# One core, one decoder layer: operand tiles at multiples of 512 bytes, output pieces crosswise in PSUM, x loaded another way

## The chip, the core and the metric

The kernel runs on one core of a Trainium2 chip. A core has TensorE (PE in the rows, with its weight loads as PEld), VectorE (DVE), ScalarE (ACT), GpSimd (POOL) and SyncE (SP); here SyncE only issues DMA transfers, and ScalarE has a DMA queue of its own. The metric is the device time of one execution in microseconds, as the median of several runs.

## What is computed

One layer of a hybrid decoder on 256 tokens of 1024 features. All inputs of the five mixer branches come from one product `h = x @ w_in + b_in`; the branches' gated outputs are merged, projected and normalized.

```python
h = x @ w_in + b_in                       # (256, 12690), split into a, b, c, d, e, z, merge
o_a = moba_attention(aq, ak, av)          # 6 heads of 64, causal at this length
o_b = dilated_mixture(bqk, bv)            # three dilations, one softmax
o_c = forgetting_attention(cq, ck, cv, log_sigmoid(c_f))
o_d = rms(gated_delta_rule(conv(d_qkv), beta, g)) * gdn_norm_w
o_e = memory_cross_attention(e_q, layer_norm(mem), w_mem_kv)
o = stack([o_a, o_b, o_c, o_d, o_e]) * silu(z)
y = sum(sigmoid(merge_logits) * einsum('bsnc,ncd->bsnd', o, w_branch), axis=2)
out = layer_norm(2 ** 0.25 * x + y @ w_out, ln_g, ln_b)
```

## The kernel before

Every large product is made of three matmuls in the type float32r: each operand is split into a part `hi` (rounded by ScalarE, L123) and a rest `lo` (a subtraction on VectorE, L124), and the products hi x hi, hi x lo and lo x hi are summed in PSUM (`mm3`, L126; every such matmul carries line L128). The tokens are kept split for the whole program in `xhi` and `xlo` (128 partitions, 8 chunks of features, 256 tokens, L140).

Weights come in units of up to 1024 columns of 4 bytes per partition (`Unit`, L163): a DMA into one of five `raw` buffers, a split into one of four `hi` and four `lo` buffers, then the matmuls. The loop at L1120 walks the units in the order of `ORDER` and keeps some loads and splits ahead. In a feature-major unit (`fm_unit`) the weights are the stationary operand and 256 tokens of xhi or xlo stream past (rows `mm<-xhi,hi`). In a token-major unit (`tm_block`) the weights stream, 384 or 402 columns, past stationary tokens (rows `mm<-hi,xhi`). The merge units stream a branch's gated output, an `f` tile of pool `f3`; the unit `mk` streams the normalized memory, in a `big` tile. Attention, convolution and the delta rule run as side streams that are stepped between the units.

The program's first block is the token-major product with `wcs` (value of branch c and its scalars). It loads and splits x piece by piece beside its own weights (`load_x` L278, `split_x` L286); x goes through two of the five `raw` buffers, all on SyncE's queue. The constants that its evacuation needs (`vcb`, `bcol` and others, `consts` at L303) are issued as a side stream among them. Matmul results of this kind lie in three `mm` buffers in PSUM.

The last product, with `w_out`, has five pieces: for token half t = 0 two of 512 columns, for t = 1 one of 512 and two of 256 (`PC`, L1021). Two `lg` tiles of two banks each take the first four (L1036: tile t holds both pieces of t), an `mm` buffer the fifth. `finish` (L1050) ends each piece with its last 15 matmuls, adds the residual on VectorE (L1071) and takes statistics (L1072); `norm` (L1054) then normalizes and stores a token half.

What stands where in memory follows from the order in which the pools are made: `cpool` with xhi, xlo and all constants first, then `wpool` (raw, hi, lo), `f3`, `big` and `sp`. In the program as built xhi and xlo start 128 bytes past a multiple of 512, and raw, hi, lo, f3 and big tiles 192 past. The order of instructions on an engine is made by a scheduler from dependencies and program order; `keep` pins an instruction to its place in program order.

Of the kernel before, what the change touches and what calls it, by code (L numbers as in the profile page):

```python
# [15 lines left out]
P = 128  # L16
S = 256
# [58 lines left out]
@with_exitstack  # L76
def kernel(ctx: ExitStack, tc: tile.TileContext, T: dict, out: bass.AP):
    nc = tc.nc
    cpool = ctx.enter_context(tc.tile_pool(name="cpool", bufs=1))
    wpool = ctx.enter_context(tc.tile_pool(name="wpool", bufs=3))  # L80
    f3 = ctx.enter_context(tc.tile_pool(name="f3", bufs=16))
    big = ctx.enter_context(tc.tile_pool(name="big", bufs=2))
    sp = ctx.enter_context(tc.tile_pool(name="sp", bufs=4))
    ps = ctx.enter_context(tc.tile_pool(name="ps", bufs=2, space=bass.MemoryType.PSUM))
    dr = ctx.enter_context(tc.tile_pool(name="dr", bufs=1, space=bass.MemoryType.DRAM))
# [6 lines left out]
    def nm(s):  # L92
        uid[0] += 1
        return f"{s}_{uid[0]}"

    def bigt(shape, dt=F32):
        return big.tile(shape, dt, tag="big", name=nm("big"))
# [7 lines left out]
    def ct(name, shape, dt=F32):  # L105
        return cpool.tile(list(shape), dt, name=name)
# [7 lines left out]
    def lgps():  # L114

        return pst("lg", (P, 2, 512), 2)
# [2 lines left out]
        return pst("av", shape, 1)  # L119


    def split(hi, lo, src):
        A_.activation(hi, src, AF.Copy)  # L123
        V_.tensor_tensor(lo, src, hi.bitcast(F32), op=ALU.subtract)  # L124

    def mm3(pt, lh, ll, rh, rl, first, last, pin=False):  # L126
# [10 lines left out]
    HR = (slice(0, 64), slice(64, 128))  # L137


    xhi, xlo = ct("xhi", (P, KD, S), F32R), ct("xlo", (P, KD, S), F32R)  # L140
    cst = ct("cst", (P, C_N))
    vb, vcb = ct("vb", (P, 2, BW)), ct("vcb", (P, BW + 18))
    bcol = ct("bcol", (P, T["bcol"].shape[1]))
# [19 lines left out]
    class Unit:  # L163
# [7 lines left out]
        def load(self):  # L171
            self.r = wpool.tile([P, 1024], F32, tag="raw", name=nm("raw"), bufs=NRAW)
            for i, p in enumerate(self.parts):
                if self.before is not None:
                    self.before[0](i, len(self.parts))
                nc.sync.dma_start(self.r[:, p], self.src[:, p])

        def split(self):
            self.h = wpool.tile([P, 1024], F32R, tag="hi", name=nm("hi"), bufs=NHI)
            self.l = wpool.tile([P, 1024], F32R, tag="lo", name=nm("lo"), bufs=NHI)  # L180
            for i, p in enumerate(self.parts):
                if self.before is not None:
                    self.before[1](i, len(self.parts))
                split(self.h[:, p], self.l[:, p], self.r[:, p])

    def need(name):
        while name is not None and name not in done:
# [88 lines left out]
    xraw = {}  # L276

    def load_x(i, j, n):  # L278
        if i % 2 == 0 and j == 0:
            xraw["t"] = wpool.tile([P, 4, S], F32, tag="raw", name=nm("raw"), bufs=NRAW)  # L280
        w = 2 // n
        o = 2 * i + w * j
        xraw[i, j] = xraw["t"][:, o % 4:o % 4 + w]
        nc.sync.dma_start(xraw[i, j], T["xT"][:, o:o + w])

    def split_x(i, j, n):  # L286
        w = 2 // n
        o = 2 * i + w * j
        split(xhi[:, o:o + w], xlo[:, o:o + w], xraw[i, j])

    def evac_c(p, t):
        if t == 0:
# [10 lines left out]
    def consts():  # L303
        for _ in range(CW):
            yield 1
        nc.sync.dma_start(vcb, T["vcb"].to_broadcast([P, BW + 18]))
        nc.sync.dma_start(bcol, T["bcol"])
        nc.sync.dma_start(cw, T["convw"])
        nc.sync.dma_start(adt, T["adt"].to_broadcast([P, 12]))
        nc.sync.dma_start(cst[:, :C_MA], T["cst"][:, :C_MA])  # L310
        flag("consts")


# [6 lines left out]
    def scalars():  # L320

        yield from wait("sc")
        nc.sync.dma_start(cst[:, C_MA:], T["cst"][:, C_MA:])
        nc.sync.dma_start(gnw, T["gnw"])
        nc.sync.dma_start(mgb, T["mgb"])
        nc.sync.dma_start(vb, T["vb"].to_broadcast([P, 2, BW]))

        V_.tensor_scalar(cwh, cw, 0.5, None, op0=ALU.mult)
        hb = bcol[:, 3 * len(FM):]
        V_.tensor_scalar(hb, hb, 0.5, None, op0=ALU.mult)  # L330
        for n, f in [("z" + i, 0.5) for i in BR] + list(QSCALE.items()):
            i = FM.index(n) * 3
            V_.tensor_scalar(bcol[:, i:i + 3], bcol[:, i:i + 3], f, None, op0=ALU.mult)
        flag("bias")
        yield
        a, lp = ct("a", (P, 2, 12)), ct("lp", (P, 2, 12))
        e, s1, s2, ea = ct("e", (P, 24)), ct("s1", (P, 24)), ct("s2", (P, 24)), ct("ea", (P, 6))
        for t in range(2):
            V_.tensor_scalar(a[:, t, 0:6], sc[:, t, 0:6], -1.0, None, op0=ALU.mult)
            V_.tensor_tensor(a[:, t, 6:12], sc[:, t, 6:12], adt[:, 6:12], op=ALU.add)  # L340
        af, lpf = a.rearrange("p t c -> p (t c)"), lp.rearrange("p t c -> p (t c)")
        V_.scalar_tensor_tensor(e, af, -1.0, af, op0=ALU.mult, op1=ALU.max)
        A_.activation(beta, sc[:, :, 12:18], AF.Exp, scale=-1.0)
        A_.activation(ea, adt[:, 0:6], AF.Exp)
        yield
        A_.activation(e, e, AF.Exp, scale=-1.0)
        V_.tensor_scalar(beta, beta, 1.0, None, op0=ALU.add)
        V_.reciprocal(beta, beta)
        V_.tensor_scalar(ea, ea, -1.0, None, op0=ALU.mult)
        yield  # L350
        V_.tensor_scalar(s1, e, 2.0, None, op0=ALU.add)
        V_.reciprocal(s1, s1)
        V_.tensor_tensor(s1, s1, e, op=ALU.mult)
        V_.tensor_tensor(s2, s1, s1, op=ALU.mult)
        V_.tensor_scalar(lpf, s2, 2.0 / 17, None, op0=ALU.mult)
        for n in (15, 13, 11, 9, 7, 5, 3):
            V_.scalar_tensor_tensor(lpf, lpf, 2.0 / n, s2, op0=ALU.add, op1=ALU.mult)
        V_.scalar_tensor_tensor(lpf, lpf, 2.0, s1, op0=ALU.add, op1=ALU.mult)
        V_.scalar_tensor_tensor(lpf, af, 0.0, lpf, op0=ALU.max, op1=ALU.add)
        yield  # L360

        for t in range(2):
            V_.tensor_scalar(fg[:, t, 0:6], lp[:, t, 0:6], -1.0, None, op0=ALU.mult)
            V_.tensor_tensor(lp[:, t, 6:12], lp[:, t, 6:12], ea, op=ALU.mult)
            V_.tensor_scalar(fg[:, t, 6:12], lp[:, t, 6:12], MAGIC, -MAGIC, op0=ALU.add, op1=ALU.add)
            V_.tensor_tensor(fg[:, t, 12:18], lp[:, t, 6:12], fg[:, t, 6:12], op=ALU.subtract)
        yield BURST

        lg = lgps()
        pt, p2 = lg[:, 0, :36].rearrange("p (t c) -> p t c", t=2), lg[0:18, 1, :S]  # L370
        keep(PE.matmul(pt[:, 0], K(C_TRI), fg[:, 0], start=True, stop=True))
        keep(PE.matmul(pt[:, 1], K(C_ONE), fg[:, 0], start=True, stop=False))
        keep(PE.matmul(pt[:, 1], K(C_TRI), fg[:, 1], start=False, stop=True))
        keep(PE.matmul(p2, fg[:, 0], K(C_TRI, 256), start=True, stop=False))
        keep(PE.matmul(p2[:, P:], fg[:, 1], K(C_TRI), start=False, stop=True))
        yield
        V_.tensor_scalar(ngt, pt, -1.0, None, op0=ALU.mult)
        grow = ct("grow", (18, S))
        V_.tensor_copy(grow, p2)
        R["gscr"] = dr.tile([18, S], F32, name="gscr")  # L380
        yield
        nc.sync.dma_start(R["gscr"], grow)
        flag("scalars")
# [635 lines left out]
    def out_units():  # L1019
# [12 lines left out]

        def chunk(u, k, t):
            if k == 0 and t == 0:
                lgs = [lgps() for _ in range(2)]
                fin["p"] = [[lg[:, i] for i in range(2)] for lg in lgs]  # L1036
                fin["p"][1].append(mmps((P, 512)))
                warm = spt("warm", (P, 1), bufs=1)
                A_.activation(warm, yhl[2][0][:, 1, 0:1].bitcast(F32), AF.Sqrt, scale=0.0, bias=0.0)
            if k < 3:  # L1040
                for i in range(len(PC[t])):
                    out_mm(u, k, t, i, k == 0, False)
            elif t == 0:
                late.append((u, k))
# [5 lines left out]
        def finish():  # L1050
# [3 lines left out]
            def norm(t):  # L1054
                V_.bn_aggr(mv[:, t], st2[t].rearrange("p c s -> p (c s)"))
                rs = rstd[:, t:t + 1]
                V_.tensor_scalar(rs, mv[:, t, 1:2], LN_EPS, None, op0=ALU.add)
                A_.activation(rs, rs, AF.Sqrt)
                V_.reciprocal(rs, rs)
                for c, cs in enumerate((slice(0, 512), slice(512, 1024))):  # L1060
                    o = xres[:, t, cs]
                    V_.scalar_tensor_tensor(o, o, mv[:, t, 0:1], lngb[:, 0, cs], op0=ALU.subtract, op1=ALU.mult)  # L1062
                    V_.scalar_tensor_tensor(o, o, rs, lngb[:, 1, cs], op0=ALU.mult, op1=ALU.add)  # L1063
                    (nc.sync, nc.scalar)[c].dma_start(out[t * P:(t + 1) * P, cs], o)
# [148 lines left out]
```

## Time and profile before

| | us |
|---|---|
| median of 3 runs (468.28 to 470.16) | 469.86 |
| the profiled execution | 469.32 |
| its span, first to last instruction | 467.2 |
| TensorE busy | 449.9 |
| VectorE busy | 328.1 |
| ScalarE busy | 265.5 |

A row of the profile names line, engine, operation and tiles as out<-in. Matmuls overlap in their pipeline, so the duration of one (some 280 ns) says little; what counts is the step from one start to the next. The granted clock is 0.994 of full speed over the whole span.

### The profile page before, as it was taken

The numbers are of one execution on the slowest core, as the hardware profiler recorded it, in microseconds if no ns is written. First come the engines' busy times: TensorE is split into PE (matmuls) and PEld (weight loads), VectorE is DVE, ScalarE is ACT, GpSimd is POOL, SyncE is SP. The second block draws the span as 40 slices with busy tenths as digits, with TensorE's granted clock in tenths as the row PEclk, the third lists the DMA queues.
The fourth block names the chain that finished last, engine by engine and source line by source line (L and its number), as shares of the span: only waits on it lengthen the run. The fifth ranks groups of instructions, "written<-read, shape, count | busy, mean of one in ns | idle before, by whom it ended". The sixth has DMA issues, their size and how long they took to land. (4 is left out here: it accounts for less than half of the span.)

```text
span 467.2 us, 10262 instructions
## 1 busy us (share of the span) xinstructions
PE 449.9 (96%) x4039; PEld 425.0 (91%) x4039; DVE 328.1 (70%) x757; ACT 265.5 (57%) x520; POOL 30.6 (7%) x36
## 2 busy tenths in 40 slices
PE   6999999999999999999999989999989999999993
PEld 3999999999998999999999989988989999999963
DVE  4799998877797535564655689895676565587746
ACT  5466685765666644444434976694684654475600
POOL 0000020010000000000000112100022112200000
PEclk9899999999999999999999999999999999999999
DMA  7978577555445545566434165564765445678202
GB/s 253 380 246 255 164 225 252 159 178 173 125 130 160 152 125 172 176 202 183 125 109 126 60 176 182 173 193 152 250 201 184 145 150 148 190 234 278 91 0 90
DMA packets 35051, 81.38 MB, mean 174 GB/s; under 512 B 8970, under 2 KB 17468, under 8 KB 34876
## 3 DMA queue, kind: packets, MB, share of 16 engines
q1 hardware_dynamic: 34715, 80.22, 55.8%
q8 instruction: 31, 0.51, 0.4%
q10 hardware_dynamic: 288, 0.52, 0.3%
q14 instruction: 17, 0.13, 0.1%
HBM read 79.37 MB, written 1.36 MB: 173 GB/s over the span
## 5 line engine op out<-in xcount | busy, mean ns | idle before, releaser
L124 DVE TENSOR_TENSOR lo<-raw,hi 128x1024 fp32r<-128x1024 f32 (+4 forms) x163 | 169.3, 1040 | 83.4 <-ACT hi L123 80.8
L128 PE MATMUL mm<-xhi,hi 128*128 128x256 f32 x776 | 219.5, 283 | 1.2 <-DVE yt L993 1.2
L128 PE MATMUL mm<-xhi,lo 128*128 128x256 f32 x776 | 216.1, 279 | 1.3 <-DVE lo L124 1.3
L128 PE MATMUL mm<-xlo,hi 128*128 128x256 f32 x776 | 216.5, 279 | 0.0
L123 ACT ACTIVATE hi<-raw 128x1024 fp32r<-128x1024 f32 (+4 forms) x163 | 146.0, 899 | 111.9 <-PE mm L128 83.5
L128 PEld LDWEIGHTS mm<-xhi,hi 128*128 128x128 f32 x776 | 146.3, 189 | 5.8 <-issue 2.7
L128 PEld LDWEIGHTS mm<-xhi,lo 128*128 128x128 f32 x776 | 145.8, 188 | 1.8 <-DVE lo L124 1.7
L128 PEld LDWEIGHTS mm<-xlo,hi 128*128 128x128 f32 x776 | 146.0, 188 | 0.8 <-issue 0.8
L128 PE MATMUL mm<-f,hi 128*128 128x256 f32 x240 | 44.7, 282 | 0.7 <-ACT th L976 0.7
L994 POOL TENSOR_TENSOR yacc<-yacc,yt 128x256 f32<-128x256 f32 x24 | 24.4, 1018 | 280.0 <-DVE yt L993 275.2
L128 PEld LDWEIGHTS mm<-f,hi 128*128 128x128 f32 x240 | 36.6, 188 | 1.6 <-ACT th L976 1.3
L128 PE MATMUL mm<-f,lo 128*128 128x256 f32 x120 | 33.7, 281 | 0.0
L128 PEld LDWEIGHTS mm<-f,lo 128*128 128x128 f32 x120 | 22.6, 188 | 0.0
L128 PE MATMUL mm<-hi,xhi 128*128 128x384 f32 (+1 forms) x48 | 16.6, 363 | 2.1 <-ACT hi L123 2.1
L135 PE MATMUL lg<-f,f 64*128 64x256 f32 (+2 forms) x192 | 18.5, 354 | 0.0
L976 ACT ACTIVATE th<-mm,bcol 128x256 f32<-128x256 f32 x40 | 18.5, 462 | 0.0
L768 ACT ACTIVATE pr<-pr,mm 128x128 f32<-128x128 f32 (+1 forms) x36 | 15.9, 443 | 4.5 <-DVE mm L759 4.5
L128 PE MATMUL mm<-lo,xhi 128*128 128x384 f32 (+1 forms) x48 | 17.3, 360 | 0.4 <-DVE lo L124 0.4
L128 PE MATMUL mm<-hi,xlo 128*128 128x384 f32 (+1 forms) x48 | 17.0, 354 | 0.0
L123 ACT ACTIVATE f<-og 128x256 fp32r<-128x256 f32 x12 | 4.9, 416 | 19.3 <-DVE og L695 15.3
L705 ACT ACTIVATE f<-mm,bcol 128x256 f32<-128x256 f32 x33 | 15.1, 456 | 0.0
L135 PEld LDWEIGHTS lg<-f,f 64*128 64x128 f32 (+1 forms) x192 | 12.5, 186 | 2.6 <-issue 0.9
(221 smaller groups left out, 529.9 us busy)
## 6 DMA issues: line engine op xcount, KB each, us to landing
raw<-in_wf_dram SPq DMA_DIRECT2D x60, 512.0 KB, 4.3
raw<-in_wm_dram SPq DMA_DIRECT2D x40, 512.0 KB, 4.0
raw<-in_wb_dram SPq DMA_DIRECT2D x40, 192.0 KB, 2.5
raw<-in_wt_dram SPq DMA_DIRECT2D x12, 384.0 KB, 3.5
raw<-in_wo_dram SPq DMA_DIRECT2D x8, 512.0 KB, 4.1
gr<-gscr SPq DMA_DIRECT2D x12, 128.0 KB, 3.5
raw<-in_wcs_dram SPq DMA_DIRECT2D x3, 402.0 KB, 5.6
raw<-in_mem_dram SPq DMA_DIRECT2D x2, 512.0 KB, 4.8
```

The source lines that it names most:

```text
L123: A_.activation(hi, src, AF.Copy)
L124: V_.tensor_tensor(lo, src, hi.bitcast(F32), op=ALU.subtract)
L128: ins = PE.matmul(pt, l, r, start=start, stop=stop)
L135: keep(PE.matmul(pt, l, r, start=start, stop=stop))
L705: A_.activation(R[name][:, m], p, AF.Identity, bias=b, scale=1.0 if scale is None else scale)
L768: A_.activation(l[:, sl], l[:, sl], AF.Exp, bias=mms[x][:, t:t + 1], scale=-1.0, accum_out=sm_[x][:, t, g:g + 1])
L976: A_.activation(th, p, AF.Tanh, bias=bcol[:, i:i + 1], scale=0.5)
L994: (V_ if last else G_).tensor_tensor(yacc[:, d], yacc[:, d], yt, op=ALU.add)
```

## The change

It moves pools and tiles. A new pool `pad` of 96 words comes first, then xhi and xlo in a pool of their own, then `wpool`, `f3` and `big`, and only then `cpool`. With this every tile of raw, hi, lo, f3 and big, and xhi and xlo, starts at a multiple of 512 bytes; the tiles of `sp` don't.

x is loaded into one `big` tile instead of `raw` buffers; its first two pieces are issued on ScalarE's queue. The loads of x, of the units of the first block and of the constants, and ScalarE's half of the first block's splits, are pinned in program order.

The first four output pieces lie crosswise: piece i of token half t in bank t of tile i. And half of one normalization (t = 0, c = 1) goes to ScalarE and GpSimd, with its store on ScalarE's queue.

```diff
-    cpool = ctx.enter_context(tc.tile_pool(name="cpool", bufs=1))
+    pad = ctx.enter_context(tc.tile_pool(name="pad", bufs=1))
+    xpool = ctx.enter_context(tc.tile_pool(name="xpool", bufs=1))
     wpool = ctx.enter_context(tc.tile_pool(name="wpool", bufs=3))
     f3 = ctx.enter_context(tc.tile_pool(name="f3", bufs=16))
     big = ctx.enter_context(tc.tile_pool(name="big", bufs=2))
+    cpool = ctx.enter_context(tc.tile_pool(name="cpool", bufs=1))
...
-    xhi, xlo = ct("xhi", (P, KD, S), F32R), ct("xlo", (P, KD, S), F32R)
+    pad.tile([P, 96], F32, name="pad")
+    xhi, xlo = [xpool.tile([P, KD, S], F32R, name=n) for n in ("xhi", "xlo")]
...
     def load_x(i, j, n):
-        if i % 2 == 0 and j == 0:
-            xraw["t"] = wpool.tile([P, 4, S], F32, tag="raw", name=nm("raw"), bufs=NRAW)
+        if i == 0 and j == 0:
+            xraw["t"] = bigt([P, KD, S])
         w = 2 // n
         o = 2 * i + w * j
-        xraw[i, j] = xraw["t"][:, o % 4:o % 4 + w]
-        nc.sync.dma_start(xraw[i, j], T["xT"][:, o:o + w])
+        xraw[i, j] = xraw["t"][:, o:o + w]
+        keep((nc.scalar if i == 0 else nc.sync).dma_start(xraw[i, j], T["xT"][:, o:o + w]))
...
-        nc.sync.dma_start(vcb, T["vcb"].to_broadcast([P, BW + 18]))
+        keep(nc.sync.dma_start(vcb, T["vcb"].to_broadcast([P, BW + 18])))
...
                 lgs = [lgps() for _ in range(2)]
-                fin["p"] = [[lg[:, i] for i in range(2)] for lg in lgs]
+                fin["p"] = [[lg[:, t_] for lg in lgs] for t_ in range(2)]
...
                     o = xres[:, t, cs]
+                    if t == 0 and c == 1:
+                        nmr = ct("nmr", (P, 1))
+                        V_.tensor_scalar(nmr, rs, mv[:, t, 0:1], -1.0, op0=ALU.mult, op1=ALU.mult)
+                        A_.activation(o, o, AF.Identity, scale=rs, bias=nmr)
+                        G_.tensor_tensor(o, o, lngb[:, 0, cs], op=ALU.mult)
+                        G_.tensor_tensor(o, o, lngb[:, 1, cs], op=ALU.add)
+                        nc.scalar.dma_start(out[t * P:(t + 1) * P, cs], o)
+                        continue
```

Two places show the new order of instructions; from some 70 us on to the tail it stays as it was, and before that the side streams stand a few rows earlier or later among the units. The first is SyncE's queue at the program's start; `in_xT` is x, `in_wcs` the first block's weights, `in_wf` those of the feature-major units. Before:

```order
L284 DMA raw_105<-in_xT_dram 128x256
L176 DMA raw_104<-in_wcs_dram 128x402
L284 DMA raw_105<-in_xT_dram 128x256
L176 DMA raw_104<-in_wcs_dram 128x402
L284 DMA raw_105<-in_xT_dram 128x512
L176 DMA raw_110<-in_wcs_dram 128x804
L284 DMA raw_114<-in_xT_dram 128x512
L176 DMA raw_113<-in_wcs_dram 128x804
L284 DMA raw_114<-in_xT_dram 128x512
L306 DMA vcb<-in_vcb_dram 128x402
L176 DMA raw_117<-in_wcs_dram 128x804
L307 DMA bcol<-in_bcol_dram 128x100
```

After:

```order
L183 DMA raw_111<-in_wcs_dram 128x402 x2
L293 DMA big_112<-in_xT_dram 128x512
L183 DMA raw_117<-in_wcs_dram 128x804
L293 DMA big_112<-in_xT_dram 128x512
L183 DMA raw_120<-in_wcs_dram 128x804
L293 DMA big_112<-in_xT_dram 128x512
L183 DMA raw_123<-in_wcs_dram 128x804
L183 DMA raw_126<-in_wf_dram 128x1024
L183 DMA raw_168<-in_wf_dram 128x1024
L183 DMA raw_188<-in_wf_dram 128x1024
L183 DMA raw_206<-in_wf_dram 128x1024
L315 DMA vcb<-in_vcb_dram 128x402
```

Two pieces of x have left for ScalarE's queue, the weights of the first block follow each other, and `vcb` stands behind four loads of `in_wf`.

The second is VectorE at the end; the number in `lg` tells the two PSUM tiles apart, and L1071 (now L1090) reads a finished piece. Before:

```order
L1071 SCALAR_TENSOR_TENSOR big_4561<-lg_6041,big_4561 128x512
L1072 BN_STATS st_6105<-big_4561 128x6
L1071 SCALAR_TENSOR_TENSOR big_4561<-lg_6041,big_4561 128x512
L1072 BN_STATS st_6105<-big_4561 128x6
L1055 BN_AGGR mv<-st_6105 128x2
L1057 TENSOR_SCALAR rstd<-mv 128x1
L1062 SCALAR_TENSOR_TENSOR big_4561<-big_4561,mv,big_4563 128x512 x2
L1059 RECIPROCAL rstd<-rstd 128x1
L1071 SCALAR_TENSOR_TENSOR big_4561<-lg_6042,big_4561 128x512
L1063 SCALAR_TENSOR_TENSOR big_4561<-big_4561,rstd,big_4563 128x512 x2
L1072 BN_STATS st_6106<-big_4561 128x6
L1071 SCALAR_TENSOR_TENSOR big_4561<-lg_6042,big_4561 128x256
```

After:

```order
L1090 SCALAR_TENSOR_TENSOR big_4567<-lg_6047,big_4567 128x512
L1091 BN_STATS st_6111<-big_4567 128x6
L1090 SCALAR_TENSOR_TENSOR big_4567<-lg_6048,big_4567 128x512
L1091 BN_STATS st_6111<-big_4567 128x6
L1065 BN_AGGR mv<-st_6111 128x2
L1067 TENSOR_SCALAR rstd<-mv 128x1
L1081 SCALAR_TENSOR_TENSOR big_4567<-big_4567,mv,big_4569 128x512
L1069 RECIPROCAL rstd<-rstd 128x1
L1082 SCALAR_TENSOR_TENSOR big_4567<-big_4567,rstd,big_4569 128x512
L1075 TENSOR_SCALAR nmr<-rstd,mv 128x1
L1090 SCALAR_TENSOR_TENSOR big_4567<-lg_6047,big_4567 128x512
L1091 BN_STATS st_6112<-big_4567 128x6
```

The pieces now alternate between the two `lg` tiles, and of the four passes of the first normalization two are left, with a small one for ScalarE's bias.

## Rows read from the trace of the kernel before

**Rows 1.** Part 1 of the page: busy us (share of the span) xinstructions.

```profile
PE 449.9 (96%) x4039; PEld 425.0 (91%) x4039; DVE 328.1 (70%) x757; ACT 265.5 (57%) x520; POOL 30.6 (7%) x36
```

**Rows 2.** The chain of waits in order of time: start us, us, what.

```profile
389.80 45.80 PE mm L128 x396
...
443.93 3.44 PE lg L128 x15
```

**Rows 3.** Timeline of TensorE near 38 us: start us, us, engine line op out<-in.

```profile
37.76 0.28 PE L128 MATMUL mm<-xhi,hi 128*128 128x256 f32 x1
...
39.12 0.28 PE L128 MATMUL mm<-xhi,hi 128*128 128x256 f32 x1
```

**Rows 4.** Timeline of TensorE near 56 us.

```profile
55.90 0.28 PE L128 MATMUL mm<-xhi,hi 128*128 128x256 f32 x1
...
56.96 0.28 PE L128 MATMUL mm<-xhi,hi 128*128 128x256 f32 x1
```

**Rows 5.** Timeline of TensorE near 312 us, unit mk.

```profile
312.54 0.40 PE L128 MATMUL mm<-big,hi 128*128 128x256 f32 x2
...
312.90 0.40 PE L128 MATMUL mm<-big,hi 128*128 128x256 f32 x2
```

**Rows 6.** Windows of L128: length, PE busy, PEld busy, PEclk, DMA share, GB/s.

```profile
11.90:13.90 2.00, 2.00 (x7) 1.97 (x7) 0.50 1.11 294
```

**Rows 7.** Timeline of TensorE in that window.

```profile
11.99 0.54 PE L128 MATMUL mm<-hi,xhi 128*128 128x402 f32 x1
...
12.99 0.54 PE L128 MATMUL mm<-hi,xhi 128*128 128x402 f32 x1
```

**Rows 8.** Groups by line and form: xcount | busy us, mean ns | idle before.

```profile
L128 PE MATMUL mm<-xhi,hi 128*128 128x256 f32 x776 | 219.5, 283 | 1.2 <-DVE yt L993 1.2
...
L128 PE MATMUL mm<-f,hi 128*128 128x256 f32 x240 | 44.7, 282 | 0.7 <-ACT th L976 0.7
...
L128 PE MATMUL lg<-hi,f 128*128 128x512 f32 x36 | 12.1, 390 | 0.0
L128 PE MATMUL mm<-hi,xhi 128*128 128x384 f32 x32 | 10.9, 342 | 0.0
```

**Rows 9.** Windows: PE, PEld, DVE, ACT, POOL busy (x), PEclk, DMA share, GB/s.

```profile
0.00:20.00 20.00, 16.28 (x67) 12.34 (x68) 11.39 (x38) 9.88 (x15) 0.20 (x4) 0.91 0.90 303
20.00:40.00 20.00, 20.00 (x175) 19.87 (x174) 19.09 (x50) 12.95 (x21) 0.00 (x0) 1.00 0.84 284
40.00:60.00 20.00, 20.00 (x174) 19.53 (x173) 18.61 (x49) 12.04 (x23) 0.93 (x1) 1.00 0.67 189
...
280.00:300.00 20.00, 20.00 (x174) 18.69 (x174) 18.89 (x54) 11.60 (x20) 4.38 (x3) 1.00 0.64 189
```

**Rows 10.** Timeline of the head; in brackets idle before, and its releaser.

```profile
4.81 0.64 PE L128 MATMUL mm<-hi,xhi 128*128 128x402 f32 x2 [0.46 <-ACT hi L123]
...
5.14 0.67 SPq L306 DMA_DIRECT2D vcb<-in_vcb_dram  x1
...
7.32 0.33 SPq L176 DMA_DIRECT2D raw<-in_wcs_dram  x1
...
12.87 0.88 ACT L123 ACTIVATE hi<-raw 128x804 fp32r<-128x804 f32 x1 [0.85 <-DMA raw<-in_wcs_dram]
...
17.68 0.35 PE L128 MATMUL mm<-lo,xhi 128*128 128x402 f32 x1
...
18.60 0.29 PE L128 MATMUL mm<-xhi,hi 128*128 128x256 f32 x1
```

**Rows 11.** Timeline of a late GpSimd add and of the tail.

```profile
406.79 0.99 POOL L994 TENSOR_TENSOR yacc<-yacc,yt 128x256 f32<-128x256 f32 x1 [2.81 <-DVE yt L993]
...
448.14 1.67 PE L128 MATMUL lg<-f,f 128*128 128x512 f32 x6 [0.79 <-DVE big L1071]
...
456.06 0.98 PE L128 MATMUL lg<-f,f 128*128 128x256 f32 x6 [0.78 <-DVE big L1071]
...
461.33 0.20 ACT L1058 ACTIVATE rstd<-rstd 128x1 f32<-128x1 f32 x1 [7.32 <-DVE rstd L1057]
```

More of the change, by code (lines that the diff above doesn't have):

```diff
@@ L119, in avps, with split @@
         return pst("av", shape, 1)
-    def split(hi, lo, src):
-        A_.activation(hi, src, AF.Copy)
+    def split(hi, lo, src, pin=False):
+        ins = A_.activation(hi, src, AF.Copy)
+        if pin:
+            keep(ins)
         V_.tensor_tensor(lo, src, hi.bitcast(F32), op=ALU.subtract)
@@ L175, in load @@
                     self.before[0](i, len(self.parts))
-                nc.sync.dma_start(self.r[:, p], self.src[:, p])
+                ins = nc.sync.dma_start(self.r[:, p], self.src[:, p])
+                if self.before is not None:
+                    keep(ins)
         def split(self):
@@ L183, in split @@
                     self.before[1](i, len(self.parts))
-                split(self.h[:, p], self.l[:, p], self.r[:, p])
+                split(self.h[:, p], self.l[:, p], self.r[:, p], self.before is not None)
     def need(name):
@@ L288, in split_x @@
         o = 2 * i + w * j
-        split(xhi[:, o:o + w], xlo[:, o:o + w], xraw[i, j])
+        split(xhi[:, o:o + w], xlo[:, o:o + w], xraw[i, j], True)
     def evac_c(p, t):
@@ L305, in consts @@
             yield 1
-        nc.sync.dma_start(vcb, T["vcb"].to_broadcast([P, BW + 18]))
[L307 to L310, printed above, removed]
+        keep(nc.sync.dma_start(vcb, T["vcb"].to_broadcast([P, BW + 18])))
+        keep(nc.sync.dma_start(bcol, T["bcol"]))
+        keep(nc.sync.dma_start(cw, T["convw"]))
+        keep(nc.sync.dma_start(adt, T["adt"].to_broadcast([P, 12])))
+        keep(nc.sync.dma_start(cst[:, :C_MA], T["cst"][:, :C_MA]))
         flag("consts")
@@ L322, in scalars @@
         yield from wait("sc")
[L323 to L326, printed above, removed]
+        keep(nc.sync.dma_start(cst[:, C_MA:], T["cst"][:, C_MA:]))
+        keep(nc.sync.dma_start(gnw, T["gnw"]))
+        keep(nc.sync.dma_start(mgb, T["mgb"]))
+        keep(nc.sync.dma_start(vb, T["vb"].to_broadcast([P, 2, BW])))
         V_.tensor_scalar(cwh, cw, 0.5, None, op0=ALU.mult)
```

## The prediction

> **What bounds the kernel now.** I read part 1 of the page first: TensorE is busy for 96% of the 467.2 us, VectorE for 70% [rows 1]. The chain of waits agrees: nearly all its long pieces are matmuls of the one helper line L128, 396 of them in a row without a wait in one piece [rows 2]. So the time is the number of matmuls times the step from one start to the next, plus the head before the stream runs and the tail behind it. The groups by line give the numbers: 3 x 776 = 2328 matmuls of 256 columns that stream xhi or xlo, 480 of 256 columns that stream f, big or hi, 144 of 384 and 72 of 512 columns, besides 48 of 402 in the head (the four rows in [rows 8] are the first of each kind, the others repeat them).
>
> The step is the point. At TensorE's upper level of 2.4 GHz, 256 columns at one a cycle would take 106.7 ns. The timeline shows four other steps. Twelve matmuls on xhi and xlo take 39.12 - 37.76 = 1.36 us, 113.3 each [rows 3]. In other stretches nine of the same kind take 1.06 us, 117.8 each [rows 4]. Three on big take 0.36 us, 120 each [rows 5]. And 15 of 512 columns take 3.44 us, 229 each, against 213.3 [rows 2]. At the lower level there is no such excess: with a granted clock of 0.50 [rows 6], three matmuls of 402 columns take 1.00 us, 333 each [rows 7], and 402 / 1.2 is 335. So the extra 7 to 16 ns are not a fixed price of an instruction; they appear where operands have to come in at twice the rate. They don't grow with the columns either (13 ns at 256, 16 at 512), so they belong to the start of an operand.
>
> Now the addresses, from the tile sizes in the order of the pools. Before, xhi and xlo start 128 bytes past a multiple of 512; raw, hi, lo, f3 and big start 192 past. What streams from 128 past takes 113.3 to 117.8, what streams from 192 past 120. This is the only thing in the trace that speaks for the first part of the change, and it has two points, none of them at 0.
>
> **The change part by part.** *Addresses.* All these tiles move to multiples of 512; sp tiles stay uneven. Nothing else in the stream changes. For the new step of 256 columns the trace gives only bounds. The lower end is 106.7, one column a cycle. The upper end is 120, the dearest row, if what helps now is the difference between the two operands' places. From 192 to 128 the step falls by 6.7 ns; one more such fall would end at 106.7, none at 113.3. I take the middle, 110. Today's mean on xhi lies between [rows 3] and [rows 4]; windows with 175 and 174 matmuls in 20 us [rows 9] make it 114.3 to 114.9, so 115. For f: the 396 in [rows 2] are twelve rounds of 24 on xhi and 9 on f; at 114.3 for the first, 108 are left with 45.80 - 32.9 = 12.9 us, 119 each. The sum: 2328 x 5 = 11.6 us, 480 x 9 = 4.3 us, and 216 wide ones x 12 (229 less 213.3 and 3.3) = 2.6 us, together 18.5. Other streams' small matmuls break the row at many places; I count seven in eight, 16.2 us.
>
> A page gives a price of its own here. The Trainium skill, "TensorE: Matmul & The Clock Gate", section Back-to-back issue gap, puts the warm step at N / 2.4 plus 2.5 ns, so 109.2 for 256 columns. By it the sum would be some 2 us more; no warm step of this trace is that short.
>
> *What VectorE gives back.* Every weight unit needs one split on ScalarE and one on VectorE. VectorE is busy 19.09 and 18.61 of 20 us in the stages behind the head and 18.89 near 290 us [rows 9]. A stream 4% faster would need these 20 us in 19.1, and VectorE can't do 19.09 us of work in that without a gap. If it reaches 97%, these windows lose 0.6, 0.1 (two like it) and 0.4 us, 1.2 in all; if the whole head gain is lost to it too, 4. I take 2.
>
> *Head.* The first two xT pieces go out on ScalarE's queue, x takes a big tile instead of two of the five raw buffers, and vcb, bcol and the other constants come behind four wf loads. Before, the 48 matmuls of the first product run from 4.81 to 18.60 us, 13.8 us; the last five of them step by (18.60 - 17.68) / 5 = 184 ns, so without waits it would be 8.8. The last wcs piece is issued at 7.32, once a raw buffer is free, behind vcb at 5.14; its split starts at 12.87 [rows 10]. Now nothing stands ahead of it but six issues on SyncE's queue, of the 0.33 to 0.67 us that the two in [rows 10] take, so it leaves near 4.0: 3.3 us sooner, the upper end. By bytes, 2.65 MB (x and all of wcs) at the 303 GB/s of the first window [rows 9] take 8.7 us; if they flow from about 2.1, an estimate, the last land at 10.8 instead of 12.9: 2.1 sooner. The cover for the late constants is the third mm buffer: the first unit of dk can run (24 x 115 = 2.8 us) before the sum with vcb must free a buffer. By the same rate vcb lands near (2.65 + 2.1 MB) / 303 + 2.1 = 17.8, and TensorE, done with wcs near 16, would ask for it near 18.8. That is just in time; each us later costs one us. ScalarE's table load now starts two issues later; the wait for the first piece of x covers that. I take 2.5 us, between 0.5 and 3.3.
>
> *Tail.* Both 512-column pieces of one token half lie in one lg tile; TensorE waits 0.79 and 0.78 us for VectorE to read the first piece before it writes the second [rows 11]. Crosswise, the next piece is in the other tile, and the tile it comes back to was left a whole piece before (3.4 us, [rows 2]): 1.6 us less, with nothing else due there. The normalization of t = 0, c = 1 leaves VectorE (two operations) for ScalarE, GpSimd and ScalarE's queue. TensorE never waits for it, so this gains nothing by itself. Its price: GpSimd's 256-column add takes 0.99 us [rows 11], so two of 512 some 4 us, from about 8 us behind the first piece's end to 12. ScalarE's store waits for that, and the last square root (461.33 [rows 11]) stands behind the store, due at about the same time. Bounds: 0 to 1 us; I take 0, since VectorE's first two passes of the last half run meanwhile and don't need the root.
>
> **Sum.** 469.3 (the profiled run, span 467.2 and 2.1 around it) - 16.2 + 2.0 - 2.5 - 1.6 = 451.0. The median of before is 0.5 above that run, so 451.5.
>
> **The rivals.** *A: only the step from 192 to 128 counts.* Then xhi is even enough already; all go to 113.3, and what is left of 117.8 goes too. 2328 x 1.7 = 4.0, 480 x 5.7 = 2.7, 216 x 9 = 1.9, seven in eight of it 7.5; with 0.5 given back, the head and the tail: 458.7. For it: 128 is a round number, and f and big alone stand off it. Against: the same place shows 113.3 and 117.8, so something is left to remove.
>
> *B: the place doesn't matter at all,* and the steps differ by what else runs. Then head and tail alone: 465.7. For it: stretches of 113.3 and 117.8 at one and the same place. Against: 120 on big, while xhi shows it in no undisturbed stretch. A rule speaks for it. The Trainium skill, "SBUF — State Buffer", section Specifications, knows lines of 16 bytes only; 128 and 192 are both whole multiples, so by that page nothing would change. The two steps at 128 and 192 disagree with it already.
>
> *C, slower: the operands get in step.* What is cheap on xhi would then be that the streamed operand (128 past) and the weights (192 past) start at different places; on big both start at 192 past and cost 120. Now all start at 0. 2328 x 5 x 7/8 = 10.2 us more, less head and tail: 476. It turns slower than before once the step on xhi is over 117. For it: [rows 5]. Against: the wcs products have weights at 128 and data at 192 or 264 past and are no cheaper: 184 ns [rows 10] against 402 / 2.4 = 167.5.
>
> **How the numbers follow.** The forecast, a step near 110, has 0.52; A 0.22, B 0.13, C 0.12. Its own range: with 106.7 throughout, 2328 x 8.3 + 480 x 12.3 + 216 x 15.5 is 28.6 us, seven in eight 25.0, and the best head against the full give-back leaves 443; the other end meets A. Keeping 8 in 10 means the forecast, A and most of B: 444 to 466. About 0.5%, 2.3 us, is what a measurement of this kernel can tell from no change. Faster by more: forecast, A and nearly half of B, 0.80; slower: C, 0.12; within it 0.08.
>
> **What would show it.** The step of three matmuls on xhi in the timeline: 0.33 us or less for the forecast, 0.34 for A, 0.36 for C; and 512 columns below 220 ns. VectorE over 96% in the windows from 20 to 80 us shows the give-back. The first 256-column matmul near 16 us, and no wait of TensorE for vcb or bcol behind it, show the head; no wait of lg for L1071 shows the tail. If the step stays and the time falls by more than 5 us, I have mispriced the head; if the step falls and the time doesn't, splits or loads have become the bound.

## The result, and the profile after

The changed kernel takes 474.2 us in the median of four runs (473.3 to 476.1) against 470.0 for the kernel before: a ratio of 1.0116, 95% interval 1.0078 to 1.0154. It is slower by some 4 us, where 451.5 was forecast. That is rival C, and nearly its number (476).

Part 1 of the page (busy us, share of the span, instructions; compare [rows 1]). TensorE does the same 4039 instructions and is busy for 9.1 us more:

```profile
PE 459.0 (97%) x4039; PEld 436.7 (93%) x4039; DVE 326.9 (69%) x756; ACT 266.4 (57%) x521; POOL 34.6 (7%) x38
```

The chain of waits of the kernel after (start us, us, what). The first row is the one that answers to [rows 2]: the same 396 matmuls, 47.70 us for 45.80, so 120.5 ns each for 115.7. The other two are the last 75 matmuls in one row without a wait:

```profile
394.17 47.70 PE mm L134 x396
...
450.22 12.02 PE lg L134 x60
462.24 1.81 PE mm L134 x15
```

The timeline of TensorE after, behind the head. The first row is the first matmul on xhi. From 16.89 to 17.25 three steps take 0.36 us, 120 ns each, where [rows 3] showed 113.3:

```profile
16.18 0.28 PE L134 MATMUL mm<-xhi,hi 128*128 128x256 f32 x1
...
16.89 0.28 PE L134 MATMUL mm<-xhi,hi 128*128 128x256 f32 x1
...
17.25 0.28 PE L134 MATMUL mm<-xhi,hi 128*128 128x256 f32 x1
```

Windows of the kernel after (PE, PEld, DVE, ACT, POOL busy with their counts, PEclk, DMA share, GB/s). 169 and 168 matmuls in 20 us stand where [rows 9] had 175 and 174, at the same granted clock. VectorE, at 19.09 us in the second window before, now has time to spare. The 1.00 of the first window, where 0.91 stood before, can't be taken as it is: a stretch at the lower level is there too (see Head below):

```profile
0.00:20.00 20.00, 17.80 (x87) 15.02 (x88) 13.56 (x42) 12.26 (x18) 0.20 (x4) 1.00 0.91 318
20.00:40.00 20.00, 20.00 (x169) 20.00 (x168) 17.74 (x48) 11.60 (x19) 0.00 (x0) 1.00 0.83 293
40.00:60.00 20.00, 20.00 (x168) 19.53 (x168) 18.08 (x48) 11.38 (x21) 0.00 (x0) 1.00 0.56 163
```

The head did what it should. SyncE's queue in the timeline after (start us, us, queue, line, transfer): the last wcs piece is out by 6.03, not 7.65, and vcb leaves at 12.13 without anyone waiting for it. TensorE is 18.60 - 16.18 = 2.4 us earlier at the first matmul on xhi, though not all of it by the loads (see Head below):

```profile
4.76 1.27 SPq L183 DMA_DIRECT2D raw<-in_wcs_dram  x1
6.08 5.99 SPq L183 DMA_DIRECT2D raw<-in_wf_dram  x4
12.13 0.42 SPq L315 DMA_DIRECT2D vcb<-in_vcb_dram  x1
```

The tail did more than it should. Timeline of TensorE after: each group of 15 with 512 columns starts 3.43 or 3.40 us behind the last, with nothing between them where [rows 11] had waits of 0.79 and 0.78:

```profile
450.05 1.55 PE L134 MATMUL lg<-f,f 128*128 128x512 f32 x6
...
453.48 1.52 PE L134 MATMUL lg<-f,f 128*128 128x512 f32 x6
...
456.88 1.52 PE L134 MATMUL lg<-f,f 128*128 128x512 f32 x6
```

In the chain of the kernel before, the last 75 matmuls run from 443.93 [rows 2] to the end of the second of these rows:

```profile
448.14 7.15 PE lg L128 x30
...
458.12 1.81 PE mm L128 x15
```

That is 16.00 us. After it is 450.22 to 464.05, 13.83 us: 2.2 less.

So the two profiled executions differ like this, in order of time:

| stretch | before, us | after, us | difference |
|---|---|---|---|
| start to the first matmul on xhi | 18.60 | 16.18 | -2.42 |
| from there to the 396 | 371.20 | 377.99 | +6.79 |
| the 396 in a row | 45.80 | 47.70 | +1.90 |
| from there to the last 75 | 8.33 | 8.35 | +0.02 |
| the last 75 | 16.00 | 13.83 | -2.17 |
| behind TensorE's end | 7.27 | 7.25 | -0.02 |
| span | 467.2 | 471.3 | +4.1 |

Head and tail give 4.6 us, the long stream loses 8.7. The question for the runs was whether equal places make the step dearer, and whether they alone do.

### The profile page after: what moved, and what is told of

It is laid out like the page before. It is cut to its first block, busy times and chain, and to the rows that moved or that the text cites. A ratio compares the mean times of both kernels' runs of the same rounds, so it can differ in the third digit from the quotient of the medians.

```text
span 471.3 us, 10268 instructions
## 1 busy us (share of the span) xinstructions
PE 459.0 (97%) x4039; PEld 436.7 (93%) x4039; DVE 326.9 (69%) x756; ACT 266.4 (57%) x521; POOL 34.6 (7%) x38
## 3 DMA queue, kind: packets, MB, share of 16 engines
HBM read 79.37 MB, written 1.36 MB: 171 GB/s over the span
## 5 line engine op out<-in xcount | busy, mean ns | idle before, releaser
L134 PE MATMUL mm<-xhi,hi 128*128 128x256 f32 x776 | 223.3, 288 | 0.7 <-DVE yt L1002 0.7
L134 PE MATMUL mm<-xhi,lo 128*128 128x256 f32 x776 | 220.2, 284 | 0.7 <-DVE lo L130 0.7
L134 PE MATMUL mm<-xlo,hi 128*128 128x256 f32 x776 | 220.3, 284 | 0.0
L134 PEld LDWEIGHTS mm<-xhi,hi 128*128 128x128 f32 x776 | 148.5, 191 | 5.2 <-issue 2.7
L134 PEld LDWEIGHTS mm<-xhi,lo 128*128 128x128 f32 x776 | 148.6, 191 | 1.1 <-DVE lo L130 1.1
L134 PEld LDWEIGHTS mm<-xlo,hi 128*128 128x128 f32 x776 | 148.6, 191 | 0.8 <-issue 0.8
```

What stands on the lines that cost most here:

```text
L134: ins = PE.matmul(pt, l, r, start=start, stop=stop)
```

## The experiments

The theories. **Distance**: what counts is how far the weights start past the operand that streams; 64 bytes, as on xhi before, is cheap, and equal places are dear. **Place**: what counts is where the streamed operand starts within 512 bytes, and 128 is better than 0 and 192. **Neither**: the pool order, the pinned loads or the pieces made the loss.

All kernels but e11 are the changed kernel with pads in the pools: `pad` ahead of xhi and xlo, and new pools `pw` ahead of `wpool` (raw, hi, lo), `pf` ahead of `f3` and `big`, `pc` ahead of `cpool`, so that the constants keep their place within 512 bytes. The fences hold for each kernel the row of its chain of waits with the 396 matmuls: 288 on xhi and xlo, 108 on f. All these rows show the same instructions, so their lengths compare directly. Means of steps given without a row are from the starts of neighbouring matmuls in the trace named. "Distance" is that of the weights past the operand.

**e1, the old places.**

```diff
-    pad.tile([P, 96], F32, name="pad")
+    pw.tile([P, 16], F32, name="pw")
+    pc.tile([P, 80], F32, name="pc")
```

> The changed kernel with the operand tiles back at their old places within 512 bytes (xhi and xlo 128 past a multiple, raw, hi, lo, f3 and big 192 past); pool order, head, pieces crosswise and normalization stay changed. If the places made the loss: the step of 256 columns on xhi falls from 120 ns back to 113.3 to 117.8, the chain's 396 matmuls take about 46 us again, and the time is 470 less the head's 2.4 and the tail's 1.6, about 466. If the places do nothing and the pool order, the pinning or the pieces made the loss: the step stays 120 and the time 474.

466.2 us, ratio to before 0.9927 (0.9896 to 0.9958). The chain, and twelve steps in the timeline of TensorE (31.41 - 30.05 = 1.36 us, 113.3 each):

```profile
388.67 45.80 PE mm L135 x396
```

```profile
30.05 0.28 PE L135 MATMUL mm<-xhi,hi 128*128 128x256 f32 x1
...
31.41 0.28 PE L135 MATMUL mm<-xhi,hi 128*128 128x256 f32 x1
```

The 396 take 45.80 us again, to the hundredth. The places made the whole loss, 474.2 - 466.2 = 8.0 us, and head, pieces and normalization together are worth 3.2 us against the 469.4 of before beside these runs (3.8 against the 470.0 above). "Neither" is out.

**e11, the places alone.** The kernel before, with weights, f3 and big moved to the place of xhi and nothing else.

```diff
+    pw = ctx.enter_context(tc.tile_pool(name="pw", bufs=1))
     wpool = ctx.enter_context(tc.tile_pool(name="wpool", bufs=3))
...
+    pw.tile([P, 112], F32, name="pw")
```

> The kernel before with one change alone: the weight, f3 and big tiles moved by 448 bytes, so that they stand 128 past a multiple of 512, as xhi does; pool order, head and tail as before. If the equal places are the whole loss: 120 ns flat on xhi, and 470 + 8 = 478 us. If the loss needs the new order of the pools or the pinned loads: 470.

478.4 us, ratio 1.0178 (1.0152 to 1.0205). The chain:

```profile
396.31 47.70 PE mm L129 x396
```

One pad of 448 bytes makes the tuned kernel 8.1 us slower. It doesn't matter that the common place is 128 here and 0 in the changed kernel.

**e2, the distance kept; e3, the place kept.** In e2 xhi stands at 0 and the weights at 64; in e3 everything stands at 128.

```diff
     pad.tile([P, 96], F32, name="pad")
+    pw.tile([P, 16], F32, name="pw")
+    pc.tile([P, 112], F32, name="pc")
```

> The changed kernel with xhi and xlo at multiples of 512 bytes, but raw, hi, lo, f3 and big 64 bytes past one: the distance from streamed operand to weights is +64 as before the change, the places are new. If the distance between the two operands counts: 113.3 to 117.8 ns a step on xhi, time near 466. If the place of the streamed operand counts (128 past is good): still 120 ns, near 474.

```diff
-    pad.tile([P, 96], F32, name="pad")
+    pc.tile([P, 96], F32, name="pc")
```

> All operand tiles, streamed ones and weights, 128 bytes past a multiple of 512: distance 0, but xhi at its old place. If the distance counts: 120 ns a step everywhere, 474 us. If the place of the streamed operand counts: 113.3 ns on xhi and also on f, and a time below 466.

e2 took 466.0 us, e3 475.0 (one run each). Their chains:

```profile
388.41 45.80 PE mm L136 x396
```

```profile
395.53 47.70 PE mm L134 x396
```

That separates the two theories, by a single run of each and by the trace: with the distance kept and the place changed the step is the old one, with the place kept and the distance gone it is the dear one. "Place", on which the forecast was built, is out.

**e4, weights 256 past** xhi and f.

```diff
     pad.tile([P, 96], F32, name="pad")
+    pw.tile([P, 64], F32, name="pw")
+    pf.tile([P, 64], F32, name="pf")
```

> xhi, xlo, f3 and big at multiples of 512 bytes, raw, hi and lo 256 past one: a distance of 256 bytes in either direction, for the token-major products as well as for the feature-major ones and the merge. If the distance counts and more of it helps more: a step below 113.3 ns, towards 106.7, on xhi and on f, and a time of 445 to 460. If only a small positive distance helps, or the place of the streamed operand counts: 120 ns, 474 us.

473.3 us (one run), the chain as at distance 0:

```profile
394.15 47.70 PE mm L136 x396
```

More distance doesn't help more, and 256 looks like 0.

**e5 to e8, other distances.** For xhi 128, 32, -64 and 192; for f 64, 96, 16 and 128.

```diff
     pad.tile([P, 96], F32, name="pad")
+    pw.tile([P, 32], F32, name="pw")
+    pf.tile([P, 112], F32, name="pf")
+    pc.tile([P, 112], F32, name="pc")
```

> xhi and xlo at multiples of 512 bytes, weights 128 past one, f3 and big 64 past: weights 128 bytes past xhi, and 64 past f. If a positive distance helps and more of it helps more: a step below 113.3 ns on xhi, and a time of some 455 to 462. If only a narrow range around 64 helps: 120 on xhi, near 474 less some 1.5 us for f. On f both say 113 to 118, where the kernel with everything at one place shows 120.

```diff
+    pw.tile([P, 8], F32, name="pw")
+    pf.tile([P, 104], F32, name="pf")
+    pc.tile([P, 16], F32, name="pc")
```

> Weights 32 bytes past xhi, and 96 past f3 and big. If the gain grows with the distance from 0 to 64: about 116 to 117 ns a step on xhi, near 470. If it is a matter of lying in another unit of 64 bytes: 120 on xhi, 474, and 113 on f, since 96 lies past 64. If 32 is already enough: 113.3 on xhi, 466.

```diff
+    pw.tile([P, 112], F32, name="pw")
+    pf.tile([P, 124], F32, name="pf")
+    pc.tile([P, 20], F32, name="pc")
```

> Weights 64 bytes ahead of xhi (448 past a multiple of 512 against 0), and 16 past f3 and big. If only the size of the distance counts: 113.3 ns on xhi, 466. If its sign counts: 120, 474, as the token-major products, whose weights stood 64 ahead of what streamed, show 173 for 384 columns before and after. On f, 16 bytes give 120 if a unit of 64 bytes decides, and 118 to 119 if the gain grows with the distance.

```diff
+    pw.tile([P, 48], F32, name="pw")
+    pf.tile([P, 96], F32, name="pf")
+    pc.tile([P, 112], F32, name="pc")
```

> Weights 192 bytes past xhi, and 128 past f3 and big. If more distance helps more, up to less than 256: at most 113.3 ns on xhi and on f, 455 to 466. If only a narrow range around 64 helps: 120 on both, 474.

They took 471.4, 470.6, 468.9 and 470.1 us, one run each. The chains, in this order:

```profile
392.67 47.04 PE mm L137 x396
```

```profile
391.75 46.99 PE mm L137 x396
```

```profile
389.94 47.15 PE mm L137 x396
```

```profile
391.07 46.92 PE mm L137 x396
```

All lie between the dear 47.70 and the cheap 45.80; none is below the old places. Six steps in e7's timeline of TensorE take 0.70 us, some 117:

```profile
29.95 0.28 PE L137 MATMUL mm<-xhi,hi 128*128 128x256 f32 x1
...
30.65 0.28 PE L137 MATMUL mm<-xhi,hi 128*128 128x256 f32 x1
```

So the sign counts: 64 ahead is worth less than 64 past, though not nothing, which neither side of the expectation had. Over the whole trace of e7 the steps between neighbouring starts on xhi and xlo are 117 or 118 ns in 1824 of 2235 cases, and in e8, at 192, in 1822: -64 and 192 are the same, as 0 and 256 were. At 32 and at 128 the steps scatter from 115 to 123.

**e9, 256 more.** If the distance counts by its rest over 256, weights 320 past xhi and 64 past f must be cheap on both.

```diff
     pad.tile([P, 96], F32, name="pad")
+    pw.tile([P, 80], F32, name="pw")
+    pf.tile([P, 112], F32, name="pf")
+    pc.tile([P, 64], F32, name="pc")
```

> xhi and xlo at multiples of 512 bytes, weights 320 past one, f3 and big 256 past: weights 320 bytes past xhi and 64 past f. If the distance counts only by what is left over 256 (as the twin results at 192 and at 448, and at 0 and 256, say): 113.3 to 117.8 ns a step on xhi as at 64, 113 to 118 on f, and 464 to 466 us. If the plain distance or a unit of 512 counts: 120 on xhi, 474.

466.1 us, ratio 0.9913 (0.9887 to 0.9939). The chain:

```profile
388.99 45.11 PE mm L137 x396
```

It came out as the rest over 256 says. The row is 0.69 us below 45.80. Mean steps in the 396, in ns:

| | before | after and e11 | e9 and e10 |
|---|---|---|---|
| on xhi and xlo | 114.1 | 120.0 | 113.4 |
| on f | 117.8 | 120.0 | 113.3 |

So f, with its weights 64 past, gives 108 x 4.5 ns = 0.49 us. The other 0.2 is on xhi: in before, the first three steps behind each nine on f take 121, 122 and 116 ns, in e9 they don't.

The table shows one thing more. In before, f and its weights stand at equal places, yet f takes 117.8 and not 120. The nine of a round come behind matmuls on xhi at 113 and step by 112 to 121; in after, behind xhi at 120, nearly all step by 120. So a step depends on what ran just before it too.

**e10, the best places.** Weights 64 past both xhi and f.

```diff
     pad.tile([P, 96], F32, name="pad")
+    pw.tile([P, 16], F32, name="pw")
+    pf.tile([P, 112], F32, name="pf")
```

> xhi, xlo, f3 and big at multiples of 512 bytes, weights 64 past one, so 64 past xhi and past f alike; head, pieces crosswise and normalization as in the changed kernel. By the distance: xhi as in the kernel before (113.3 to 117.8 ns), f some 2 to 3 ns cheaper than there on 385 matmuls, about 1 us: 465 us, faster than both kernels. If the places of f and xhi hinder each other: no better than 466.

465.5 us in six runs (464.4 to 466.7), ratio 0.9900 (0.9879 to 0.9921): faster than both kernels. The chain:

```profile
389.94 45.10 PE mm L136 x396
```

The advantage over e1 and e9 is within their scatter. What is shown is the gain over before and, in the chain, the 0.70 us on f and on the matmuls right behind it.

**e12, lo apart.** Which of two neighbours collides, a matmul with its own weights or with those of the next?

```diff
+    pw = ctx.enter_context(tc.tile_pool(name="pw", bufs=1))
     wpool = ctx.enter_context(tc.tile_pool(name="wpool", bufs=3))
+    pl = ctx.enter_context(tc.tile_pool(name="pl", bufs=1))
+    lpool = ctx.enter_context(tc.tile_pool(name="lpool", bufs=3))
...
-            self.l = wpool.tile([P, 1024], F32R, tag="lo", name=nm("lo"), bufs=NHI)
+            self.l = lpool.tile([P, 1024], F32R, tag="lo", name=nm("lo"), bufs=NHI)
...
     pad.tile([P, 96], F32, name="pad")
+    pw.tile([P, 16], F32, name="pw")
+    pl.tile([P, 112], F32, name="pl")
```

> xhi, xlo, f3, big and lo at multiples of 512 bytes, raw and hi 64 past one. The matmuls come in threes, weights hi, hi, lo, against xhi, xlo, xhi. If a matmul is dear when its own weights stand at the place of its operand: the third of each three takes 120 and the others 113 to 118. If it is dear because the weights of the next matmul are loaded while it streams: the second of each three takes 120. In both cases the time lies between 466 and 474, near 469.

470.6 us (one run); the chain:

```profile
391.74 46.83 PE mm L137 x396
```

Neither came true. In all three positions of a three the median step is 117 or 118 ns; no position pays 120 or gets 113. One dear neighbour takes the cheap step from all three. Which pair collides stays open, and so does what in the memory or in TensorE does it: the runs show a rule of distances, not its cause.

**The wider matmuls hardly followed.** Their distances changed with the pads as well: in the token-major products the weights stood 64 ahead in before, equal in after, 64 past in e7. Over all fourteen traces the mean step of 384 columns is 173 to 176 ns, that of 402 columns at the full clock 181 to 184, that of 512 columns 228 to 233, and equal places were not the dearest. So the rule is shown for the steps of 256 columns alone.

## Why the prediction was wrong, point by point

**What bounds the kernel** held: steps of the long stream decide. A tail shortened by 2.2 us and a head shortened by 2.4 were outweighed by some 5 ns a step.

**The addresses, the step that failed.** It is the sentence "From 192 to 128 the step falls by 6.7 ns; one more such fall would end at 106.7, none at 113.3", with 110 taken between. It read the two points as places of one operand. They were two pairs: xhi at 128 with weights at 192, and big at 192 with weights at 192. e2 and e3 show that the pair decides. The term was -16.2 us and measured +8.0 (after against e1) and +8.1 (e11 against before). Both readings fitted [rows 3] and [rows 5] equally well, since equal places stood nowhere in before but at 192. So a chance of 0.12 for C beside 0.74 for two forms of the other reading had nothing in the rows to rest on.

The bounds failed with it: the upper end, 120, was the true value, and against the 115 of before it makes a loss, yet it went into the middle of a gain. None of the distances tried gave a step near 110; the cheapest row of 396 is 45.10 us, 113.9 each. Here the Trainium skill, "TensorE: Matmul & The Clock Gate", section Back-to-back issue gap, gives N / 2.4 plus 2.5 ns, 109.2 for 256 columns, as the gap of an isolated matmul, and says that a stream with weight loads is spaced otherwise. The stream here differs from 109.2 in every run, and the measurement decides: 113.3 at the best distance, 120 at equal places.

The argument made against C, that the wcs products with weights at 128 and data at 192 are no cheaper, was no evidence. The steps of these wider products hardly follow the distance: 402 columns take 184 ns with the weights 64 past (e7), 182 with them 64 ahead (before), 184 at equal places (after). So they could speak neither for C nor against it.

**f and the wide matmuls.** 480 x 9 and 216 x 12 ns were counted as gains. f, at equal places before and after, rose by 2.2 ns in the 396, behind a dearer xhi, and fell by 4.5 only in e9 and e10. Groups of 15 with 512 columns take 3.40 us against 3.44, 227 ns a step: nothing near the 220 that was named as the sign.

**Rival C** had the mechanism and the signs: 10.2 us for xhi, less head and tail, 476. Its step was right too: in the 396 a matmul on xhi loses some 6 ns, and between the head and these rows the mean step goes from 114.9 in before to 119.7 in e11, 4.8 ns on some 1900 of them, 9.1 us. But e11 gets to the 396 only 396.31 - 389.80 = 6.51 us later. In that stretch TensorE is idle for 371.20 - 366.51 = 4.7 us in before and for 377.80 - 375.29 = 2.5 in e11 (windows 18.60:389.80 and 18.50:396.30): a slower stream waits less for the other engines. C had no term for that, and it is the give-back with its sign turned. **B** is e1, which undoes just the places: forecast 465.7, measured 466.2.

**VectorE's give-back** was a right mechanism that had no gain to take back in the changed kernel, whose stream is slower. In e1, which keeps the head's lead, it shows. The groups of waits of TensorE for before and e1 (us in total, times, longest) have the merge's `yt` in the stage near 280 us, where VectorE is full [rows 9]:

```profile
PE mm L128 <- DVE yt L993: 1.2, 1, 1.2
```

```profile
PE mm L135 <- DVE yt L1004: 2.1, 1, 2.1
```

The earlier TensorE arrives, the longer it waits; of the head's 2.4 us, 389.80 - 388.67 = 1.1 are left at the 396. I had 2 us given back; it was some 1.2 for the head's gain alone, 0.9 of it in this wait.

**Head**: -2.5 forecast, -2.4 found, no wait for vcb as said. The number was in part luck. I had worked it out from the last wcs piece, but TensorE waits for that piece in neither kernel: before, its split starts at 12.87 [rows 10], and the last wait in this product ends at 10.73, at the 15th of the 48 matmuls:

```profile
10.73 0.45 PE L128 MATMUL mm<-lo,xhi 128*128 128x402 f32 x1 [0.40 <-DVE lo L124]
```

After, the same matmul starts at 9.80:

```profile
6.13 0.54 PE L134 MATMUL mm<-lo,xhi 128*128 128x402 f32 x1
...
8.47 0.52 PE L134 MATMUL mm<-hi,xlo 128*128 128x402 f32 x1
...
9.80 0.45 PE L134 MATMUL mm<-lo,xhi 128*128 128x402 f32 x1
```

So up to there the new order of loads and splits brought 0.9 us. The other 1.5 is in the 34 matmuls from there on, 18.60 - 10.73 = 7.87 us before and 16.18 - 9.80 = 6.38 after, and nearly all of that is the granted clock, which I hadn't named. Before, a stretch at the lower level, 0.50, falls among them [rows 6], with steps of some 334 ns [rows 7]. After, steps of (8.47 - 6.13) / 7 = 334 ns stand ahead of them, where they cost little: e1, with the same head and no such steps, has its first matmul on xhi at 16.24. The profile shows no granted clock below 1.00 there; the steps do.

**Tail**: -1.6 forecast, -2.2 found. The difference is mis-sized, not a new mechanism: a group of 15 takes 3.40 us in an unbroken row, while the two behind the first wait took 7.15 in the chain before, 3.6 each, and the two of 256 columns behind the second wait lost about as much again. The normalization on ScalarE and GpSimd cost nothing, as taken. Timeline of GpSimd, ScalarE and its queue after:

```profile
461.50 1.29 POOL L1077 TENSOR_TENSOR big<-big,big 128x512 f32<-128x512 f32 x1 [48.76 <-ACT big L1076]
462.87 1.28 POOL L1078 TENSOR_TENSOR big<-big,big 128x512 f32<-128x512 f32 x1
```

```profile
464.18 0.35 ACTq L1079 DMA_DIRECT2D out_dram<-big  x1
465.45 0.20 ACT L1068 ACTIVATE rstd<-rstd 128x1 f32<-128x1 f32 x1 [4.02 <-DVE rstd L1067]
```

The store is out at 464.53, 0.9 us ahead of the root that it could have delayed. The two passes of 512 columns take 2.6 us, not the estimated 4.

## What to carry to other kernels

Before operand tiles are moved to round addresses, look at pairs: take from the built program where the weights and the streamed operand of each matmul start, and sort the steps in the trace by the difference. In this kernel, float32r with 256 columns, weights 64 bytes past the operand, by the rest over 256, were cheapest and equal places dearest. Its wider matmuls hardly followed the distance, and other types weren't tried. And where two rows allow two readings of opposite sign, a forecast should not put most of its chance on one of them: the trace then holds no answer, and a pad of some bytes, tried alone, gives it.

## What the runs showed of the hardware that I had not expected

The step of these float32r matmuls of 256 columns at the full clock depends on the distance between the two operands, by the rest over 256 bytes: 120 ns at 0 (1933 of the 2235 steps between neighbours on xhi and xlo in the changed kernel), 113.3 or 117 to 118 at 64, 117 to 118 at 192, and scattered from 115 to 123 at 32 and 128. With 384, 402 and 512 columns the mean step moved by some 2% at most, and equal places were not the dearest.

At 64 there are two steps at one and the same place, and one of them lasts until something breaks the row. Windows of before, e1 and e10 (PE, PEld, DVE, ACT, POOL, PEclk, DMA share, GB/s) have 347, 351 and 340 matmuls in the same 40 us:

```profile
20.00:60.00 40.00, 40.00 (x347) 39.39 (x346) 37.70 (x98) 25.00 (x42) 0.93 (x1) 1.00 0.75 236
```

```profile
20.00:60.00 40.00, 40.00 (x351) 39.52 (x350) 37.55 (x108) 23.99 (x40) 0.34 (x1) 1.00 0.74 234
```

```profile
20.00:60.00 40.00, 40.00 (x340) 39.53 (x340) 36.86 (x102) 23.59 (x40) 0.00 (x0) 1.00 0.71 230
```

In before, the step goes from 118 to 113 ns at 25 us, behind two steps of 0.22 us; in e10 it stays at 117 to 118 for these 40 us. What chooses between the two wasn't tried.

In the profiled run of e10 the wait for `yt` cost more than its 1.8 us. Its windows there:

```profile
275.00:280.00 5.00, 3.25 (x18) 2.23 (x16) 4.77 (x9) 2.39 (x4) 0.99 (x1) 0.85 0.23 54
280.00:285.00 5.00, 5.00 (x34) 4.17 (x34) 3.89 (x12) 2.96 (x5) 1.04 (x1) 0.81 0.80 299
```

TensorE was busy for 3.25 of 5 us, and the granted clock fell to 0.85 and 0.81 in these windows; in e1, with a wait of 2.1 us at the same place, its windows stayed at 1.00. So the longer of the two waits left the clock alone and the shorter was followed by a fall; what decides wasn't tried.
